# First four blocks of a layer side by side, their weights split ahead of the norm, and no weight split on GpSimd

## The chip, the cores and the metric

The kernel runs on one core of one Trainium2 chip. A core has a matrix engine (TensorE, PE), a vector engine (VectorE, DVE), an activation engine (ScalarE, ACT), a general engine (GpSimd, POOL) and an engine that only issues DMAs here (SyncE, SP). Each works through its own list of instructions in order and waits on semaphores for the others. The metric is the device time of one execution in microseconds (us), as a median of several runs. A difference of less than 0.2%, about 5 us, is not told from no change.

## The reference

Four layers of a transformer-like network run over 512 tokens of width 1024, in float32. In short:

```python
# first_block: two layers, each with a LayerNorm behind the mixer and behind the FFN
h = layer_norm(ALPHA * h + s5_mixer(h), ...)              # state-space model, then a GLU
h = layer_norm(ALPHA * h + swiglu_ffn(h, w_gu, w_down))   # hidden width 2816
h = layer_norm(ALPHA * h + stick_breaking_mixer(h), ...)  # 16 heads
h = layer_norm(ALPHA * h + swiglu_ffn(h, w_gu, w_down))
# second block: two layers with an RMS norm ahead of each part
h = h + mixer_even(rms_norm(h))      # gated MLP beside dilated attention
h = h + conv_ffn(rms_norm(h))        # SwiGLU FFN with a causal convolution of 3 taps
h = h + mixer_odd(rms_norm(h))       # gated linear attention, 4 heads
h = h + conv_ffn(rms_norm(h))
```

## The kernel before, in words

The activations stand transposed: 8 tiles `v[m]` of 128 features by 512 tokens. Eight stages follow each other: ssm, ffn0, stick, ffn1, even (gated MLP, then dilated attention), conv0, gla, conv1.

Float32 accuracy comes from splitting. An activation tile is `xh` (rounded) plus `xl` (the rest); a weight block of 128x1024 is `wh` plus `wl`. `mm3` takes three matmuls for each of 8 tiles k: `xh` with `wh`, `xl` with `wh`, `xh` with `wl`. An output block of 128x512 thus needs 24 matmuls of 512 columns, or 48 of 256 if it is worked half by half.

`weight()` makes a block ready: SP loads 512 KB into `wr` (2 buffers), ACT rounds it to `wh` (L207), and a subtraction gives `wl` (L210). The subtraction runs on DVE, apart from 44 blocks for which it runs on GpSimd: all of dilated attention's (`lo_pool`), and the first few after each norm, counted by `AHEAD`. `wh` and `wl` have 4 buffers each.

`linear()` runs a layer's input blocks. With `split_first=4` the first four are worked half by half: all of block 0's first half, then block 1's, and so on, and then the second halves. The convolution FFNs have no such start. `out_blocks()` runs the output blocks and the norm: the last `nl` blocks half by half, and behind each half its norm. For LayerNorm that is `ln_half`: `colsum` sums the columns on PE, DVE works out the inverse root of the variance in some 14 instructions on `small` tiles (`rstd`, L363 to L370), `spread` makes `diag` operands (L394) which PE multiplies by ones to bring the row to all partitions (L396), and then each of 8 tiles is subtracted from and multiplied (L410, L411), scaled and shifted by ACT, rounded to `xh` by ACT (L214), and its rest `xl` taken by DVE (L215). For the RMS norm (`rms_half`) only the scale's row is made, and it is applied where the next layer's blocks are read out; the next tiles are made ahead of it by `scaled` (L352, L353).

The order of the instructions on each engine is set by a scheduler at build time, except that the SSM stage's steps follow a written list, `SSM_STEPS`, and the attentions lists of their own. In `SSM_STEPS` a letter is a kind of step and a digit the tile or group: P powers of the state matrix; m, q, n, N products of powers and inputs on DVE; A, B, C, X matmuls or their preparation; W and w the load and split of a GLU weight; G the GLU's matmuls.

Of the kernel before, what the change touches and what calls it, by code (L numbers as in the profile page):

```python
# [98 lines left out]
class Kern:  # L99
    def __init__(self, tc, ins, out, ctx):  # L100
        self.tc, self.nc, self.i, self.out = tc, tc.nc, ins, out
        self.g = ctx.enter_context(tc.tile_pool(name="glob", bufs=1))
# [4 lines left out]
        self.lo_pool = False
        self.nw = 0
        self.nb = 0
        self.boundary = ()  # L110
# [151 lines left out]
    def out_blocks(self, blocks, xh, xl, kind, g=None, b=None, alpha=1.0, rg=None, nl=1):  # L262
# [1519 lines left out]
```

## Time and profile before

| what | value |
|---|---|
| median of 3 runs | 2511.8 us (2509.65 to 2515.39) |
| the profiled execution's own time | 2507.85 us |
| its span | 2506.1 us |
| granted TensorE clock, mean of the span | 0.988 of full speed |
| GpSimd busy | 117.9 us |
| ScalarE busy | 1004.9 us |

The profile is of one execution; its own time is 3.95 us below the median of the runs. The span is the time from its first to its last instruction. Busy time counts an engine's instructions; the clock is that which TensorE was granted, 1.00 being 2.4 GHz and 0.50 being 1.2 GHz.

### The profile page before, as it was taken

The numbers are of one execution on the slowest core, as the hardware profiler recorded it, in microseconds if no ns is written. First come the engines' busy times: TensorE is split into PE (matmuls) and PEld (weight loads), VectorE is DVE, ScalarE is ACT, GpSimd is POOL, SyncE is SP. The second block draws the span as 40 slices with busy tenths as digits, with TensorE's granted clock in tenths as the row PEclk, the third lists the DMA queues.
The fourth block names the chain that finished last, engine by engine and source line by source line (L and its number), as shares of the span: only waits on it lengthen the run. The fifth ranks groups of instructions, "written<-read, shape, count | busy, mean of one in ns | idle before, by whom it ended". The sixth has DMA issues, their size and how long they took to land. (4 is left out here: it accounts for less than half of the span.)

```text
span 2506.1 us, 31148 instructions
## 1 busy us (share of the span) xinstructions
PE 2417.5 (96%) x12296; PEld 2006.6 (80%) x12300; DVE 1445.8 (58%) x2512; ACT 1004.9 (40%) x1552; POOL 117.9 (5%) x106
## 2 busy tenths in 40 slices
PE   5899999999999999999998899999999999999999
PEld 4788888888877788888876678888888888788888
DVE  8955733343777884333377787656435667666531
ACT  4853422322555643232244454333324554333321
POOL 0000100000100010000023202000000000100000
PEclk9899999999999999999999999999999999999999
DMA  3332232233211113223322112222332122222332
GB/s 104 71 102 97 68 101 96 97 93 95 84 60 60 45 58 118 98 95 94 94 82 76 46 39 91 94 101 94 94 99 78 68 85 76 84 97 96 97 108 73
DMA packets 99378, 213.52 MB, mean 85 GB/s; under 512 B 44528, under 2 KB 45168, under 8 KB 99232
## 3 DMA queue, kind: packets, MB, share of 16 engines
q1 hardware_dynamic: 99232, 211.53, 26.5%
q8 instruction: 97, 1.59, 0.3%
q14 instruction: 49, 0.40, 0.1%
HBM read 207.04 MB, written 2.10 MB: 83 GB/s over the span
## 5 line engine op out<-in xcount | busy, mean ns | idle before, releaser
L207 ACT ACTIVATE wh<-wr 128x1024 fp32r<-128x1024 f32 (+1 forms) x385 | 400.3, 1041 | 1010.8 <-PE mm L230 392.6
L210 DVE TENSOR_TENSOR wl<-wr,wh 128x1024 fp32r<-128x1024 f32 (+1 forms) x341 | 408.8, 1199 | 450.4 <-ACT wh L207 449.5
L230 PE MATMUL mm<-xl,wh 128*128 128x512 f32 (+1 forms) x1144 | 439.9, 385 | 0.0
L229 PE MATMUL mm<-xh,wh 128*128 128x512 f32 (+1 forms) x1144 | 439.2, 387 | 0.2 <-ACT scr L1309 0.2
L231 PE MATMUL mm<-xh,wl 128*128 128x512 f32 (+1 forms) x1144 | 438.4, 384 | 0.0
L230 PE MATMUL acc<-xl,wh 128*128 128x512 f32 (+1 forms) x888 | 336.0, 379 | 6.6 <-DVE xl L215 6.4
L229 PE MATMUL acc<-xh,wh 128*128 128x512 f32 (+1 forms) x888 | 337.2, 380 | 1.2 <-ACT xh L214 1.0
L231 PE MATMUL acc<-xh,wl 128*128 128x512 f32 (+1 forms) x888 | 336.0, 378 | 0.0
L229 PEld LDWEIGHTS mm<-xh,wh 128*128 128x128 f32 x1144 | 216.5, 190 | 42.7 <-issue 2.8
L230 PEld LDWEIGHTS mm<-xl,wh 128*128 128x128 f32 x1144 | 217.3, 190 | 40.9 <-issue 0.7
L231 PEld LDWEIGHTS mm<-xh,wl 128*128 128x128 f32 x1144 | 217.2, 190 | 40.6 <-issue 0.4
L230 PEld LDWEIGHTS acc<-xl,wh 128*128 128x128 f32 x888 | 167.2, 189 | 38.4 <-DVE xl L215 7.6
L210 POOL TENSOR_TENSOR wl<-wr,wh 128x1024 fp32r<-128x1024 f32 (+1 forms) x44 | 105.1, 2391 | 1901.6 <-ACT wh L207 1839.4
L229 PEld LDWEIGHTS acc<-xh,wh 128*128 128x128 f32 x888 | 167.6, 189 | 32.6 <-ACT xh L214 1.4
L231 PEld LDWEIGHTS acc<-xh,wl 128*128 128x128 f32 x888 | 167.5, 189 | 31.0
L229 PE MATMUL acc<-hh,wh 128*128 128x512 f32 (+1 forms) x396 | 145.0, 366 | 1.0 <-DVE v L327 1.0
L229 PE MATMUL mm<-hh,wh 128*128 128x512 f32 (+1 forms) x396 | 145.0, 366 | 0.5 <-DVE v L327 0.5
L230 PE MATMUL acc<-hl,wh 128*128 128x512 f32 (+1 forms) x396 | 145.2, 367 | 0.0
L230 PE MATMUL mm<-hl,wh 128*128 128x512 f32 (+1 forms) x396 | 144.8, 366 | 0.0
L231 PE MATMUL mm<-hh,wl 128*128 128x512 f32 (+1 forms) x396 | 144.7, 365 | 0.0
L231 PE MATMUL acc<-hh,wl 128*128 128x512 f32 (+1 forms) x396 | 144.7, 365 | 0.0
L229 PEld LDWEIGHTS acc<-hh,wh 128*128 128x128 f32 x396 | 74.6, 188 | 13.5 <-DVE v L327 1.4
(468 smaller groups left out, 3693.1 us busy)
## 6 DMA issues: line engine op xcount, KB each, us to landing
wr<-down_dram SPq DMA_DIRECT2D x64, 448.0 KB, 3.3
wr<-gu_g_dram SPq DMA_DIRECT2D x44, 512.0 KB, 3.2
wr<-gu_u_dram SPq DMA_DIRECT2D x44, 512.0 KB, 3.2
wr<-gate_dram SPq DMA_DIRECT2D x44, 512.0 KB, 3.2
wr<-up_dram SPq DMA_DIRECT2D x44, 512.0 KB, 3.2
wr<-down_dram SPq DMA_DIRECT2D x32, 512.0 KB, 3.5
wr<-sb_qkv_dram SPq DMA_DIRECT2D x24, 512.0 KB, 3.2
wr<-glu_dram SPq DMA_DIRECT2D x16, 512.0 KB, 3.3
```

The source lines that it names most:

```text
L207: nc.scalar.activation(hi[:, :cols], raw[:, :cols], AF.Copy)
L210: (nc.gpsimd if pool else nc.vector).tensor_sub(lo[:, :cols], raw[:, :cols], hi[:, :cols])
L229: nc.tensor.matmul(ps[:, c0:c1], wh[:, s], xh[k][:, c0:c1], start=st, stop=False)
L230: nc.tensor.matmul(ps[:, c0:c1], wh[:, s], xl[k][:, c0:c1], start=False, stop=False)
L231: nc.tensor.matmul(ps[:, c0:c1], wl[:, s], xh[k][:, c0:c1], start=False, stop=en)
```

## The change

GpSimd splits no weights any more: all `wl` come from DVE. `FIRST` names each stage's first four blocks (none for gla). `prepare()` loads and splits them ahead of their layer: where the last blocks go half by half, two of the four ahead of these and two in the norm between its rows and its tiles; where `nl` is 0, all four behind the last block. `wh` and `wl` get 5 buffers each. `mm3_side` works four blocks side by side: for each tile k the three matmuls of each of the four, in halves (`parts=2`) for ffn0, ffn1 and stick, over the full 512 columns for the convolution FFNs, which had no joint start before. Blocks 3 and 4 take `aux` banks of PSUM. `ln_half` becomes `ln_rows` and `ln_apply`, the first half applied in two parts; ACT makes `xh` straight from the scaled tile. The output blocks of even and gla are all full-width (`nl` 2 to 0). The list of SSM steps is new; three tags lose a buffer (`scr` 9 to 8, `tst` 4 to 3, `BC` 4 to 3).

```diff
 SSM_STEPS = (
-    "q1 i0 i1 W2 q0 W3 m0 P0 A0 m1 K0 A0 P1 A1 K0 Z0 A0 K1 P2 D1 A1 D0 a1 D2 P3 i2 A1 K1 b1 n0 K1 i3 B1 D3 c1 K0 "
...
+    "P0 i0 i1 W0 m0 W2 P1 q0 P2 A0 m1 K0 A0 P3 K0 A0 q1 K0 i2 B0 e0 m2 q2 A1 s0 n0 A2 K1 N0 Z0 A1 K2 n1 D0 A2 K1 "
...
-AHEAD = (4, 3, 4, 6, 7, 1, 7, 0)
+FIRST = {
+    "ffn0": [(n, 0, f) for f in (0, 1) for n in ("gu_g", "gu_u")],
+    "stick": [("sb_qkv", m) for m in (8, 0, 16, 9)],
+    "ffn1": [(n, 1, f) for f in (0, 1) for n in ("gu_g", "gu_u")],
+    "even": [("ev_v", u) for u in range(4)],
+    "conv0": [(n, 0, f) for f in (0, 1) for n in ("gate2", "up2")],
+    "conv1": [(n, 1, f) for f in (0, 1) for n in ("gate2", "up2")],
+}
...
     def scr(self, dt=F32):
-        return self.gt("scr", [P, T], dt, bufs=9)
+        return self.gt("scr", [P, T], dt, bufs=8)
...
-    def weight(self, ap, cols=1024):
-        nc = self.nc
+    def weight(self, *key, ap=None, cols=1024):
+        nc = self.nc
+        if key and key in self.early:
+            return self.early.pop(key)
         raw = self.wt("wr", F32, 2)
-        nc.sync.dma_start(raw[:, :cols], ap)
-        hi, lo = self.wt("wh", F32R, 4), self.wt("wl", F32R, 4)
+        nc.sync.dma_start(raw[:, :cols], self.i[key[0]][key[1:]] if ap is None else ap)
+        hi, lo = self.wt("wh", F32R, 5), self.wt("wl", F32R, 5)
         nc.scalar.activation(hi[:, :cols], raw[:, :cols], AF.Copy)
-        self.nw += 1
-        pool = self.lo_pool or self.nw in self.boundary
-        (nc.gpsimd if pool else nc.vector).tensor_sub(lo[:, :cols], raw[:, :cols], hi[:, :cols])
+        nc.vector.tensor_sub(lo[:, :cols], raw[:, :cols], hi[:, :cols])
         return hi, lo
+
+    def prepare(self, n):
+
+        for key in self.coming[:n]:
+            self.early[key] = self.weight(*key)
+        self.coming = self.coming[n:]
...
+    def mm3_side(self, pss, ws, xh, xl, parts=1):
+
+        nc = self.nc
+        n = T // parts
+        for c0 in range(0, T, n):
+            c = slice(c0, c0 + n)
+            for k in range(NM):
+                s = slice(k * P, (k + 1) * P)
+                for ps, ((wh, wl), _, _) in zip(pss, ws):
+                    nc.tensor.matmul(ps[:, c], wh[:, s], xh[k][:, c], start=k == 0, stop=False)
+                    nc.tensor.matmul(ps[:, c], wl[:, s], xh[k][:, c], start=False, stop=False)
+                    nc.tensor.matmul(ps[:, c], wh[:, s], xl[k][:, c], start=False, stop=k == NM - 1)
+
+    def linear(self, blocks, xh, xl, evict, side=0, parts=1, group=1):
 
         n = len(blocks)
         i = 0
-        if split_first:
-            ws = [blocks[j]() for j in range(split_first)]
-            pss = [self.bank() for _ in range(split_first)]
-            for h in (0, 1):
-                for j in range(split_first):
-                    self.mm3(pss[j], ws[j], xh, xl, h * HALF, (h + 1) * HALF)
-            for j in range(0, split_first, group):
+        if side:
+            ws = [blocks[j]() for j in range(side)]
+            pss = [self.bank() if j < 2 else self.aux() for j in range(side)]
+            self.mm3_side(pss, [w for w, in ws], xh, xl, parts)
+            for j in range(0, side, group):
                 evict(j, pss[j:j + group])
-            i = split_first
+            i = side
...
+            if m == NM - nl - 1:
+                self.prepare(2 if nl else 4)
         last = range(NM - nl, NM)
         ws, pss = {}, {}
-        for h in (0, 1):
+        if not nl and rms:
+            for h in (0, 1):
+                self.rms_half(h, acc2)
+        for h in (0, 1) if nl else ():
             c = slice(h * HALF, (h + 1) * HALF)
             for m in last:
                 if h == 0:
@@ -339,12 +365,16 @@
                 if h == 0:
                     for m in range(NM):
                         next_tiles(m)
-                self.ln_half(h, acc1, acc2, g, b, nxh, nxl, rg)
+                    rows0 = self.ln_rows(0, acc1, acc2)
+                    self.prepare(4)
+                    self.ln_apply(0, range(4), rows0, g, b, nxh, nxl, rg)
+                else:
+                    self.ln_apply(0, range(4, NM), rows0, g, b, nxh, nxl, rg)
+                    rows1 = self.ln_rows(1, acc1, acc2)
+                    self.ln_apply(1, range(NM), rows1, g, b, nxh, nxl, rg)
             if rms:
                 self.rms_half(h, acc2)
         self.xh, self.xl = nxh, nxl
-        self.boundary = range(self.nw + 1, self.nw + 1 + AHEAD[self.nb])
-        self.nb += 1
...
-    def ln_half(self, h, acc1, acc2, g, b, nxh, nxl, rg):
-        nc, v = self.nc, self.v
-        c = slice(h * HALF, (h + 1) * HALF)
+    def ln_rows(self, h, acc1, acc2):
+
+        nc = self.nc
         d = self.colsum([acc1, acc2], (2 * h, 2 * h + 1))
         q = self.small(2)
         nc.vector.tensor_mul(q, d[:, :2], d[:, :2])
         nc.vector.scalar_tensor_tensor(q, d[:, 2:4], 1e-5, q, op0=ALU.add, op1=ALU.subtract)
-        r = self.rstd(q, 2)
-        db, rb = self.spread([d[:, :2], r])
-        for m in range(NM):
+        return self.spread([d[:, :2], self.rstd(q, 2)])
+
+    def ln_apply(self, h, ms, rows, g, b, nxh, nxl, rg):
+        nc, v = self.nc, self.v
+        c = slice(h * HALF, (h + 1) * HALF)
+        for m in ms:
             y = self.scr()[:, :HALF]
-            nc.vector.tensor_sub(y, v[m][:, c], db)
-            nc.vector.tensor_mul(y, y, rb)
+            nc.vector.tensor_sub(y, v[m][:, c], rows[0])
+            nc.vector.tensor_mul(y, y, rows[1])
             gm, bm = g[:, m:m + 1], b[:, m:m + 1]
             if rg is None:
-                nc.scalar.activation(v[m][:, c], y, AF.Identity, scale=gm, bias=bm)
-                self.split(v[m][:, c], nxh[m][:, c], nxl[m][:, c])
-                continue
+                nc.scalar.activation(nxh[m][:, c], y, AF.Identity, scale=gm, bias=bm)
             nc.scalar.activation(v[m][:, c], y, AF.Identity, scale=gm, bias=bm)
-            self.scaled(m, c, rg, nxh, nxl)
+            if rg is None:
+                nc.vector.tensor_sub(nxl[m][:, c], v[m][:, c], nxh[m][:, c])
+            else:
+                self.scaled(m, c, rg, nxh, nxl)
...
-            self.linear(blocks, self.xh, self.xl, evict, split_first=4 if conv is None else 0, group=2)
+            self.linear(blocks, self.xh, self.xl, evict, side=4, parts=2 if conv is None else 1, group=2)
...
-    BC = 4
+    BC = 3
...
-            for h in (0, 1):
-                for w, ps in zip(ws, pss):
-                    self.mm3(ps, w, xh, xl, h * HALF, (h + 1) * HALF)
+            self.mm3_side(pss, [w for w, in ws], xh, xl, 2)
...
-    def attention(self, pairs, first, project, weigh, done, mask, order, units, lo_pool=False):
-
-
-        self.lo_pool = lo_pool
...
-            self.out_linear(self.simple_blocks("ev_wo", NM), oh, ol, "rms", rg=self.nfg[0], nl=2)
+            self.out_linear(self.simple_blocks("ev_wo", NM), oh, ol, "rms", rg=self.nfg[0], nl=0)
...
-            self.out_linear(self.simple_blocks("od_wo", NM), oh, ol, "rms", rg=self.nfg[1], nl=2)
+            self.out_linear(self.simple_blocks("od_wo", NM), oh, ol, "rms", rg=self.nfg[1], nl=0)
...
-        for s in stages:
+        for n, s in enumerate(stages):
+            k.coming = FIRST.get(stages[n + 1], []) if n + 1 < len(stages) else []
```

Three pairs of excerpts show how the instructions stand on two engines. First PE at the start of ffn0: `acc` and `mm` are the PSUM banks of its first two blocks, `xh_2168` the first tile's rounded part, `wh_2454` and `wh_2460` the weights. Before:

```order
L229 MATMUL acc_2476<-xh_2168,wh_2454 128x256
L230 MATMUL acc_2476<-xl_2169,wh_2454 128x256
L231 MATMUL acc_2476<-xh_2168,wl_2455 128x256
L229 MATMUL acc_2476<-xh_2170,wh_2454 128x256
L229 MATMUL mm_2477<-xh_2168,wh_2460 128x256
L230 MATMUL mm_2477<-xl_2169,wh_2460 128x256
L230 MATMUL acc_2476<-xl_2171,wh_2454 128x256
L231 MATMUL acc_2476<-xh_2170,wl_2455 128x256
L229 MATMUL acc_2476<-xh_2172,wh_2454 128x256
L230 MATMUL acc_2476<-xl_2173,wh_2454 128x256
```

After, with the names and lines of the changed kernel (`xh_2178`, `wh_2057` and `wh_2063`):

```order
L252 MATMUL acc_2474<-xh_2178,wh_2057 128x256
L253 MATMUL acc_2474<-xh_2178,wl_2058 128x256
L254 MATMUL acc_2474<-xl_2179,wh_2057 128x256
L252 MATMUL mm_2475<-xh_2178,wh_2063 128x256
L253 MATMUL mm_2475<-xh_2178,wl_2064 128x256
L254 MATMUL mm_2475<-xl_2179,wh_2063 128x256
L252 MATMUL acc_2474<-xh_2180,wh_2057 128x256
L253 MATMUL acc_2474<-xh_2180,wl_2058 128x256
L252 MATMUL mm_2475<-xh_2180,wh_2063 128x256
L253 MATMUL mm_2475<-xh_2180,wl_2064 128x256
L254 MATMUL acc_2474<-xl_2181,wh_2057 128x256
L254 MATMUL mm_2475<-xl_2181,wh_2063 128x256
```

Block 1 ran on to its second and third tile as soon as they were there, with block 2 in the gaps. Now the blocks alternate tile by tile, and the `wl` product stands ahead of the `xl` product.

Next DVE in the norm between SSM and ffn0, around the two `diag` operands of its first half. Before:

```order
L370 SCALAR_TENSOR_TENSOR small_2209<-small_2206,small_2204 128x2
L394 TENSOR_SCALAR diag_2218<-ident_58,small_2209 128x128
L394 TENSOR_SCALAR diag_2221<-ident_58,small_2209 128x128
L410 TENSOR_TENSOR scr_2224<-v_739,aux_2211 128x256
L411 TENSOR_TENSOR scr_2224<-scr_2224,aux_2211 128x256
L410 TENSOR_TENSOR scr_2230<-v_799,aux_2211 128x256
L411 TENSOR_TENSOR scr_2230<-scr_2230,aux_2211 128x256
L410 TENSOR_TENSOR scr_2236<-v_857,aux_2211 128x256
L327 TENSOR_TENSOR v_1316<-v_1316,mm_2100 128x256
L411 TENSOR_TENSOR scr_2236<-scr_2236,aux_2211 128x256
L215 TENSOR_TENSOR xl_2169<-v_739,xh_2168 128x256
L410 TENSOR_TENSOR scr_2242<-v_946,aux_2211 128x256
```

After (`wl_2237` and `wl_2243` are the lower parts of ffn0's third and fourth weight):

```order
L302 TENSOR_TENSOR acc_369_1864<-acc_369_1864,v_1240 128x256
L400 SCALAR_TENSOR_TENSOR small_2219<-small_2216,small_2214 128x2
L214 TENSOR_TENSOR wl_2237<-wr_2234,wh_2236 128x1024
L424 TENSOR_SCALAR diag_2228<-ident_58,small_2219 128x128
L424 TENSOR_SCALAR diag_2231<-ident_58,small_2219 128x128
L443 TENSOR_TENSOR scr_2246<-v_673,aux_2221 128x256
L353 TENSOR_TENSOR v_1310<-v_1310,mm_2110 128x256
L444 TENSOR_TENSOR scr_2246<-scr_2246,aux_2221 128x256
L443 TENSOR_TENSOR scr_2252<-v_738,aux_2221 128x256
L214 TENSOR_TENSOR wl_2243<-wr_2240,wh_2242 128x1024
L450 TENSOR_TENSOR xl_2179<-v_673,xh_2178 128x256
L444 TENSOR_TENSOR scr_2252<-scr_2252,aux_2221 128x256
```

A split of 128x1024 now stands right ahead of the two `diag` instructions, and another between the second tile's subtraction and the first tile's `xl`. Before, GpSimd had them.

Last PE at the entry of conv0, where even's last output block ends and the RMS norm's row is spread (`aux` from `diag`). Before, `mm_12781` is the last output block and `mm_12950` conv0's first:

```order
L231 MATMUL mm_12781<-oh_12466,wl_12778 128x256
L229 MATMUL mm_12781<-oh_12495,wh_12777 128x256
L230 MATMUL mm_12781<-ol_12496,wh_12777 128x256
L396 MATMUL aux_12839<-diag_12840,ones_1436 128x128
L396 MATMUL aux_12839<-diag_12843,ones_1436 128x128
L231 MATMUL mm_12781<-oh_12495,wl_12778 128x256
L229 MATMUL mm_12950<-xh_12537,wh_12946 128x512
L230 MATMUL mm_12950<-xl_12538,wh_12946 128x512
```

After, `mm_12906` and `acc_12907` are conv0's first two blocks:

```order
L253 MATMUL acc_12907<-xh_12652,wl_12821 128x512
L254 MATMUL acc_12907<-xl_12653,wh_12820 128x512
L252 MATMUL mm_12906<-xh_12691,wh_12814 128x512
L253 MATMUL mm_12906<-xh_12691,wl_12815 128x512
L426 MATMUL aux_12861<-diag_12862,ones_1434 128x128
L426 MATMUL aux_12861<-diag_12865,ones_1434 128x128
L411 MATMUL aux_12869<-cst_63,acc_2317_12501 128x1 x2
L254 MATMUL mm_12906<-xl_12692,wh_12814 128x512
L252 MATMUL acc_12907<-xh_12691,wh_12820 128x512
L253 MATMUL acc_12907<-xh_12691,wl_12821 128x512
L254 MATMUL acc_12907<-xl_12692,wh_12820 128x512
L252 MATMUL mm_12906<-xh_12730,wh_12814 128x512
```

The spread stood within the last output block's second half. It now stands among the full-width matmuls of the next stage's first blocks.

## Rows read from the trace of the kernel before

**Rows 1.** The page: busy time of PE and DVE over the span

```profile
PE 2417.5 (96%) x12296; PEld 2006.6 (80%) x12300; DVE 1445.8 (58%) x2512; ACT 1004.9 (40%) x1552; POOL 117.9 (5%) x106
```

**Rows 2.** Windows of 50 us: length, busy time (instructions) by engine, clock, DMA share, GB/s

```profile
50.00:100.00 50.00, 37.24 (x359) 34.24 (x358) 42.91 (x54) 35.27 (x68) 0.45 (x4) 0.86 0.31 71
250.00:300.00 50.00, 44.48 (x327) 42.66 (x326) 37.81 (x101) 24.82 (x47) 7.09 (x3) 0.93 0.13 44
300.00:350.00 50.00, 50.00 (x222) 41.43 (x221) 20.69 (x22) 16.93 (x22) 0.00 (x0) 1.00 0.36 117
900.00:950.00 50.00, 44.24 (x297) 41.37 (x296) 37.29 (x86) 27.68 (x49) 7.33 (x3) 0.93 0.19 64
1250.00:1300.00 50.00, 46.14 (x276) 39.95 (x275) 32.02 (x77) 18.05 (x31) 10.94 (x5) 1.00 0.28 94
1300.00:1350.00 50.00, 41.14 (x173) 32.01 (x171) 45.77 (x93) 27.80 (x50) 15.01 (x6) 0.94 0.22 74
```

**Rows 3.** Waits of PE: us in total, times, longest

```profile
PE aux L396 <- DVE diag L394: 11.0, 8, 2.2
...
PE acc L230 <- DVE xl L215: 6.4, 4, 2.6
...
PE aux L1227 <- ACT vnh L214: 5.0, 1, 5.0
...
PE aux L1325 <- DVE small L1318: 2.8, 2, 2.2
...
PE aux L381 <- DVE acc L281: 2.3, 1, 2.3
```

**Rows 4.** Timeline of DVE, 257 to 271 us: start, duration

```profile
258.27 2.65 DVE L394 TENSOR_SCALAR diag<-ident,small 128x128 f32<-128x128 f32 x2
...
265.06 2.42 DVE L215 TENSOR_TENSOR xl<-v,xh 128x256 fp32r<-128x256 f32 x1 [0.48 <-ACT xh L214]
...
267.40 0.41 DVE L410 TENSOR_TENSOR scr<-v,aux 128x256 f32<-128x256 f32 x1
...
268.40 2.90 DVE L215 TENSOR_TENSOR xl<-v,xh 128x256 fp32r<-128x256 f32 x2
```

**Rows 5.** Timeline of POOL, the same stretch

```profile
264.80 2.40 POOL L210 TENSOR_TENSOR wl<-wr,wh 128x1024 fp32r<-128x1024 f32 x1 [4.16 <-ACT wh L207]
...
268.34 2.34 POOL L210 TENSOR_TENSOR wl<-wr,wh 128x1024 fp32r<-128x1024 f32 x1 [1.14 <-ACT wh L207]
```

**Rows 6.** Timeline of DVE in the gated MLP, 1330 to 1350 us

```profile
1335.02 5.70 DVE L1206 TENSOR_TENSOR scr<-scr,ev_ln_g 128x512 f32<-128x512 f32 x2
...
1343.96 1.28 DVE L1206 TENSOR_TENSOR scr<-scr,ev_ln_g 128x512 f32<-128x512 f32 x2
```

**Rows 7.** Timeline of PE, 255 to 275 us: in brackets the wait before

```profile
260.78 0.71 PE L396 MATMUL aux<-diag,ones 128*128 128x128 f32 x4 [2.15 <-DVE diag L394]
...
271.02 0.39 PE L230 MATMUL acc<-xl,wh 128*128 128x256 f32 x1 [2.62 <-DVE xl L215]
```

**Rows 8.** Windows of PE alone: length, busy (instructions), clock, DMA

```profile
261.00:265.00 4.00, 4.00 (x23) 0.59 0.40 135
271.00:275.00 4.00, 3.98 (x22) 0.62 0.40 131
280.00:298.20 18.20, 17.59 (x142) 1.00 0.00 1
1350.00:1356.00 6.00, 5.80 (x24) 0.67 0.25 87
1428.00:1436.00 8.00, 8.00 (x35) 0.72 0.00 0
1540.00:1545.00 5.00, 4.67 (x18) 0.67 0.38 112
```

**Rows 9.** The page: groups of the weight split, by engine

```profile
L210 DVE TENSOR_TENSOR wl<-wr,wh 128x1024 fp32r<-128x1024 f32 (+1 forms) x341 | 408.8, 1199 | 450.4 <-ACT wh L207 449.5
...
L210 POOL TENSOR_TENSOR wl<-wr,wh 128x1024 fp32r<-128x1024 f32 (+1 forms) x44 | 105.1, 2391 | 1901.6 <-ACT wh L207 1839.4
```

More of the change, by code (lines that the diff above doesn't have):

```diff
@@ L106, in __init__ @@
         self.fresh, self.taken = [], {}
[L107 to L110, printed above, removed]
+        self.early, self.coming = {}, []
         self.consts()
@@ L231, in mm3 @@
                 nc.tensor.matmul(ps[:, c0:c1], wl[:, s], xh[k][:, c0:c1], start=False, stop=en)
-    def linear(self, blocks, xh, xl, evict, split_first=0, group=1):
+    def mm3_side(self, pss, ws, xh, xl, parts=1):
[10 more added lines that the diff above has]
+    def linear(self, blocks, xh, xl, evict, side=0, parts=1, group=1):
         n = len(blocks)
         i = 0
-        if split_first:
-            ws = [blocks[j]() for j in range(split_first)]
-            pss = [self.bank() for _ in range(split_first)]
-            for h in (0, 1):
-                for j in range(split_first):
-                    self.mm3(pss[j], ws[j], xh, xl, h * HALF, (h + 1) * HALF)
-            for j in range(0, split_first, group):
+        if side:
[3 more added lines that the diff above has]
+            for j in range(0, side, group):
                 evict(j, pss[j:j + group])
-            i = split_first
+            i = side
         while i < n:
@@ L460, in block @@
             def block(name, f):
-                return lambda: [(self.weight(self.i[name][layer, f]), 0, 8)]
+                return lambda: [(self.weight(name, layer, f), 0, 8)]
             blocks = [b for f in range(FT) for b in (block(gname, f), block(uname, f))]
@@ L484, in evict @@
                 self.split(s, hh[f], hl[f])
-            self.linear(blocks, self.xh, self.xl, evict, split_first=4 if conv is None else 0, group=2)
+            self.linear(blocks, self.xh, self.xl, evict, side=4, parts=2 if conv is None else 1, group=2)
             def dblock(m):
-                return lambda: [(self.weight(self.i[dname][layer, m][:, k0 * P:(k0 + nk) * P], nk * P), k0, nk)
+                return lambda: [(self.weight(ap=self.i[dname][layer, m][:, k0 * P:(k0 + nk) * P], cols=nk * P), k0, nk)
                                 for k0, nk in FSPLIT]
@@ L494, in simple_blocks @@
     def simple_blocks(self, name, n):
-        return [(lambda m=m: [(self.weight(self.i[name][m]), 0, 8)]) for m in range(n)]
+        return [(lambda m=m: [(self.weight(name, m), 0, 8)]) for m in range(n)]
     def vexp(self, x, sp, minus1=True):
@@ L874, in ssm @@
                                  self.ident[:, None, :].to_broadcast([P, 16, P]), AF.Copy, scale=0.0)
-            self.tst = [self.pt(f"tst{k}", [P, 8, 65]) for k in range(4)]
+            self.tst = [self.pt(f"tst{k}", [P, 8, 65]) for k in range(3)]
             for t in self.tst:
@@ L918, in ssm @@
                     elif f == "W":
-                        raw, w = self.wt("wr", F32, 2), [self.wt(n, F32R, 4) for n in ("wh", "wl")]
+                        raw, w = self.wt("wr", F32, 2), [self.wt(n, F32R, 5) for n in ("wh", "wl")]
                         self.nc.sync.dma_start(raw, self.i["glu"][(o // 2) + 8 * (o % 2)])
@@ L925, in ssm @@
                         self.nc.vector.tensor_sub(w[1], raw, w[0])
-                        self.nw += 1
                         fps[o] = self.mm()
@@ L1065, in scores, with attention @@
         return z
-    def attention(self, pairs, first, project, weigh, done, mask, order, units, lo_pool=False):
-        self.lo_pool = lo_pool
+    def attention(self, pairs, first, project, weigh, done, mask, order, units):
         st = [{} for _ in range(pairs)]
@@ L1097, in attention @@
                         done(hp, s["o"])
-        self.lo_pool = False
     def stick(self):
@@ L1152, in token_proj @@
         nc = self.nc
-        ws = [self.weight(u) for u in units]
+        ws = [self.weight(*u) for u in units]
         pss = [self.bank() for _ in range(4)]
@@ L1180, in early @@
                 self.mm3(pu[-1], w, self.xh, self.xl)
-        pv = self.token_proj([i["ev_v"][u] for u in range(4)], self.xh, self.xl)
+        pv = self.token_proj([("ev_v", u) for u in range(4)], self.xh, self.xl)
         with self.phase("big") as self.big:
@@ L1355, in first @@
                 project(hp, st[hp], n)
-        self.attention(4, first, project, weigh, done, mask, EVEN_STEPS, EVEN_UNITS, lo_pool=True)
+        self.attention(4, first, project, weigh, done, mask, EVEN_STEPS, EVEN_UNITS)
     def even(self):
@@ L1412, in gla_gate @@
         nc = self.nc
-        w = self.weight(self.i["od_ga"], P)
+        w = self.weight(ap=self.i["od_ga"], cols=P)
         ps = self.mm()
@@ L1430, in gla_values @@
         nc = self.nc
-        ws = [self.weight(self.i["od_v"][pair, u]) for u in range(4)]
+        ws = [self.weight("od_v", pair, u) for u in range(4)]
         for tb in range(4):
```

14 rows, old and new, of the table SSM_STEPS are left out of this document.

## The prediction

> **What bounds the kernel now.** I looked first at the page: TensorE (PE) is busy 96% of the span and VectorE (DVE) 58% [rows 1]. So what any change can win is PE's idle time, some 88 us of 2506, and the time that PE spends at a lower clock. The 50-us windows say where those are: a stretch in the middle of a layer holds 222 matmuls of 512 columns and PE is busy all of it, while 50–100 us (the state-space mixer), 250–300, 900–950 and 1250–1350 us hold 37 to 46 us of PE work, some at clock 0.86 to 0.94 [rows 2]. Apart from the first, these windows are layer ends: the norm needs the last block, the next layer needs the norm.
>
> The waits of PE, grouped by what ended them, name the norm's own chain: the `diag` operands of the spread 11.0 us in 8 waits, `xl` 6.4 us in 4, then `vnh` in the gated MLP 5.0, `small` in dilated attention 2.8, and others [rows 3]. All come from DVE or, as `vnh`, from ScalarE (ACT) behind DVE.
>
> Why is DVE late there? Going to its rows at one layer end: a `diag` pair takes 2.65 us at 258.27 and an `xl` 2.42 at 265.06, while the 256-wide subtract at 267.40 takes 0.41; the next `xl` pair takes 2.90 [rows 4]. GpSimd (POOL) runs a weight split at just these moments: 264.80 to 267.20 and 268.34 to 270.68 [rows 5]; each long DVE instruction ends within 0.3 us of its split's end. In the gated MLP two multiplies take 5.70 us beside POOL's two splits and 1.28 us without [rows 6]. So a split on POOL doesn't run beside DVE there: it holds a DVE instruction for about 2.0 to 2.2 us. PE waits 2.15 us for that `diag` and 2.62 for that `xl` [rows 7], and after either its granted clock is 0.59 or 0.62 for 4 us, mostly the lower level (1.2 of 2.4 GHz) [rows 8].
>
> **The change part by part.**
>
> *Splits.* 44 leave POOL (2391 ns each) and join DVE's queue (1199 ns each) [rows 9]: DVE gains 44 × 1.2 = 52.8 us of its own work. What it loses are the holds: at most 44 × 2.0 = 88 us if each split holds one instruction, as both of rows 5 do, at least nothing. I take three in four, 66 us, since some splits fall where DVE is idle or reads PSUM. DVE's load falls by some 13 us; with no hold at all it would rise by 53, and the busiest window's 45.8 of 50 us [rows 2] would be the place that feels it.
>
> The Trainium skill bears on this in both directions (Perfetto Trace Analysis, "Optimizing Scalar/DVE Operations"): where DVE is saturated, moving work to GpSimd may make sense, though the two share an SBUF read port and it might not help. The GPSIMD Engine Reference ("Key points") names the contention: DVE instructions in a 2-port mode or with two SBUF inputs. By the first half of the rule, the six splits that POOL does in 1300–1350 us would cost DVE 7 us more there, and the sum below would lose the 5 us of that place; rows 6 agree with the second half.
>
> *Layer end, LayerNorm* (first output block pairs of the next layer, 2 halves). The matmuls stay 256 wide there, and their order changes: four blocks take tile 0, then tile 1, so that PE needs one new tile for 12 matmuls, 12 × 0.124 = 1.5 us (17.59 us for 142 in 280–298 [rows 8]), where one block took 3, 0.37 us. DVE makes a tile in three instructions of 0.41 (subtract, multiply, `xl`) [rows 4], 1.25 us: PE no longer outruns it. Ahead of the `diag` now stands one DVE split, and one more among the first tiles. At SSM→ffn0, hence: of the wait of 2.15, 1.2 stay, 0.95 go; of the 2.62, 1.2 stay, 1.4 go; of the clock's loss, 4 × 0.41 + 4 × 0.38 = 3.2 us [rows 8], I take back half, 1.6, since shorter waits may still lower it. Gain 4.0; bounds: nothing (the waits only move) and all, 5.5 idle + 3.2 = 8.7. Stick→ffn1 (900–950: 5.8 idle, clock 0.93 [rows 2]) is built alike: 4.0, bounds 0 and 8.7. ffn0→stick is not among the stretches with much idle time: 0.5, bounds −1 and 1.5. The two weights split ahead of the last blocks, and the other two in the norm, replace loads that came behind it; two more buffers (`wh`, `wl`) hold them. Their DMAs keep their number and size, and the DMA share in 250–300 is 0.13 [rows 2]. The new direct ACT write of `xh` takes one step from each tile's chain and adds no instruction.
>
> *ffn1→gated MLP* (1250–1350: 3.9 + 8.9 idle [rows 2]). Waits of 2.3 (`acc`) and 5.0 (`vnh`) [rows 3] stand out. Before `vnh` the multiplies are held 5.70 − 1.28 = 4.4 us [rows 6]; with two DVE splits, 2.4, in that place, 2.0 go. Of the 2.3, 1.2 stay, 1.1 go; clock 0.67 over 6 us [rows 8] gives 1.0 of its 2.0; of the smaller waits, 5.5 us together, I take 0.9: 5. Bounds 0 and 12.
>
> *Dilated attention.* Eight splits move into DVE's in-order queue, 9.6 us, against eight holds of 2.0. PE's 2.8 us of waits for `small` [rows 3] and the 2.2 us that clock 0.72 costs over the next 8 [rows 8] are at stake, 5 us; I take half, 2.5, as the splits can stand ahead of the same chain, and 0.5 for lesser waits: 3. Bounds −1 and 6.
>
> *Conv layers' entries* (from the dilated layer and from gated linear attention). The last two output blocks go full-width. A pair of 256-wide matmuls takes 0.248 us, one 512-wide 0.225 [rows 8, 2], so 48 × 0.023 = 1.1 us per entry. The norm's chain moves under the first blocks of the next layer (PE's order: colsum, then 13 full matmuls, 2.9 us, before the spread), and the held `diag` wait (2.2 at most [rows 3]) and clock 0.67 over 5 us, 1.7 [rows 8], go: 5.0 in all. I keep 2 back for splits on DVE in the chain: 3 each, bounds 1 and 5. Half a microsecond comes from gated linear attention's own start, whose one split moves too.
>
> *SSM.* The written-out order is new, with three buffers for two tiles that had four and eight scratch tiles for nine. In 50–100 us DVE is busy 42.9 of 50 and PE 37.2 [rows 2]: DVE sets the pace, and its work is the same. Its 7.1 idle us are the bound of a gain; 1.3 us more work (one step of 1.2 us and part of a power) stands ahead of the first matmul, so +6 at best. Fewer buffers could as well double the idle time: −8. The new table lets the weight splits' loads wait behind the third output tile but drops two table switches of ACT. I take +2.
>
> *At nothing:* POOL's idle time, and the reordered product terms (`wl` before `xl`): both lie beside PE's work; if `wl` came late it would cost its 1.2 us, once per entry.
>
> **Sum:** SSM 2 + 4 + 0.5 + 4 + 5 + 3 + 3 + 3 + 0.5 = 25 us. Against the profiled execution's 2507.85 (span 2506.1, 1.75 around it) that is 2482.9. The median of the runs shown is 2511.8, 3.95 above the profiled one; the forecast as a median is 2486.8, rounded **2487**.
>
> **The rivals.**
>
> *The waits only move* (small gain). DVE executes in order: a split stands ahead of `diag` and waits for ACT's `wh`, which waits for the load. Then the layer ends and attention give nothing; conv entries 6, SSM 2, 0.5 remain: 2503. For it: DVE at 45.8 of 50. Against it: 1.2 us takes the place of 2.0 to 2.2.
>
> *All of it goes.* PE finds every tile ready: the upper bounds 8.7 + 8.7 + 1.5 + 12 + 6 + 5 + 5 + 0.5 with SSM's 2 make 49, so 2462. Against it: after the last block the chain of the norm must still run before the second half.
>
> *The clock stays low* (no change). PE now paces tile by tile with DVE, 1.5 against 1.25 us, so short waits come between groups of 12 matmuls. If these held the clock at its lower level through the first halves of four blocks at three entries, each would lose 96 × (0.21 − 0.12) = 8.6 us (rows 8: 0.124 at clock 1.00; 0.21 lies midway between 0.181, 22 in 3.98 us at 0.62, and twice 0.124), 26 in all, one more than the sum: 2513. Rows 8 show the fall after waits over 2 us, and the 0.61 us of idle in 280–298 left it at 1.00. The Trainium skill describes such a loss (TensorE: Matmul & The Clock Gate, "A second HAM failure mode: psum-queue depth-cycling"): micro-idles between groups make the clock swing. No row here shows it.
>
> *A late load stops DVE* (slower). In the norm the third and fourth weight need a raw buffer of the two; if their load lands after the split's turn, everything behind it on DVE stops: `diag`, all tiles, evictions of the blocks. At the price of the 2.62-us wait and half of 3.2 for the clock, 4.2 us twice in each of four norms, 34 us stand against 25: 2521. It decides from 3.1 us per split. For it: DVE mostly waited for ACT's `wh` before a split (449.5 of 450.4 us [rows 9]). Against: the first two loads come three blocks earlier, 16 us.
>
> **How the numbers follow.** Forecast (2477 to 2498, one of its larger terms lost or doubled): 0.64. Only moved: 0.14. All: 0.08. Clock: 0.06. Late load: 0.08. About 5 us, 0.2%, is what a measurement here can tell from no change. Faster by more: 0.64 + 0.08 + 0.10 of "only moved" = 0.82; within: 0.04 + 0.06 = 0.10; slower: 0.08. The range 2466 to 2508 holds the forecast with a larger gain in part, and "only moved", and leaves out most of the full gain and the last two.
>
> **What would show it.** Right: no DVE instruction of `diag`, `xl` or `small` over 0.8 us; `diag` and `xl` waits of PE together under 8 us (now 17.4); `vnh` near 3; DVE busy 1425 to 1445 us; windows as 250–300 with 47 or more of PE at clock 0.96 or above. Wrong: waits of PE for `wl`; DVE waiting over 2 us before a split inside a norm; PE busy below 37 us in 50–100 us; clock under 0.8 in a stretch of short waits.

## The result, and the profile after

| what | before | after |
|---|---|---|
| median | 2510.73 us (4 runs) | 2474.44 us (4 runs, 2473.41 to 2475.27) |
| ratio | | 0.9852, 95% interval 0.9835 to 0.9869 |
| profiled execution, span | 2507.85, 2506.1 | 2473.41, 2471.7 |
| clock, mean of the span | 0.988 | 0.992 |

The change takes 36 us, 1.5%. The forecast was 25 us (2487), with a range of 2466 to 2508. The range holds the result, but the narrower band of 2477 to 2498, to which the prediction gave 0.64, doesn't. On the page of the changed kernel, PE's busy time and the single group of weight splits answer to [rows 1, 9]:

```profile
PE 2405.6 (97%) x12200; PEld 1993.5 (81%) x12204; DVE 1415.8 (57%) x2544; ACT 1005.5 (41%) x1542; POOL 14.0 (1%) x61
...
L214 DVE TENSOR_TENSOR wl<-wr,wh 128x1024 fp32r<-128x1024 f32 (+1 forms) x385 | 461.7, 1199 | 448.4 <-ACT wh L213 443.9
```

DVE makes 44 splits more and is busy 30 us less. PE's idle time falls from 88.6 to 66.1 us, and its busy time by 11.9 us. The mean clock, 0.992 after 0.988, can make up about 10 of these (an estimate: 0.004 of 2500 us). The windows of the changed kernel, against [rows 2]:

```profile
50.00:100.00 50.00, 41.44 (x401) 38.28 (x401) 44.78 (x58) 41.30 (x77) 0.34 (x3) 0.90 0.43 89
250.00:300.00 50.00, 47.38 (x321) 43.92 (x321) 35.11 (x93) 29.19 (x50) 0.00 (x0) 0.97 0.21 68
900.00:950.00 50.00, 48.70 (x286) 44.15 (x286) 29.82 (x72) 26.29 (x43) 0.00 (x0) 0.93 0.25 83
1250.00:1300.00 50.00, 45.24 (x264) 37.65 (x264) 40.41 (x110) 29.04 (x60) 1.09 (x1) 1.00 0.28 85
1300.00:1350.00 50.00, 46.24 (x222) 36.86 (x222) 37.41 (x93) 24.77 (x42) 4.35 (x14) 0.93 0.26 85
```

Its waits of PE, against [rows 3]; the waits for `diag`, `xl` and `vnh`, 22.4 us there, are 4.1 here. Some waiting has moved to ACT: at the layer ends the waits for `xh` come to 5.4 us, 1.7 in the kernel before, and the 3.1 us for `scr` are new:

```profile
PE aux L91 <- DVE m L91: 24.2, 3, 21.8
PE mm L239 <- ACT scr L1338: 3.1, 1, 3.1
...
PE mm L1190 <- ACT xh L382: 2.3, 2, 2.1
PE aux L426 <- DVE diag L424: 2.0, 4, 1.0
...
PE mm L252 <- ACT xh L447: 1.9, 2, 1.0
PE acc L252 <- ACT xh L447: 1.2, 2, 0.9
...
PE acc L254 <- DVE xl L450: 0.9, 2, 0.7
PE mm L254 <- DVE xl L450: 0.9, 2, 0.7
...
PE aux L1256 <- ACT vnh L224: 0.3, 1, 0.3
```

Where did the 34.4 us of span go? The timeline of PE gives the first matmul on `zh` (SSM's output blocks), on `hh` (an FFN's output blocks) and on `oh` (output blocks of even and gla). These marks cut the span into stretches. Before:

```profile
216.18 0.39 PE L229 MATMUL acc<-zh,wh 128*128 128x512 f32 x1
...
515.96 0.39 PE L229 MATMUL acc<-hh,wh 128*128 128x512 f32 x1
...
1158.62 0.39 PE L229 MATMUL acc<-hh,wh 128*128 128x512 f32 x1
...
1482.29 0.47 PE L229 MATMUL mm<-oh,wh 128*128 128x512 f32 x1
...
1783.29 0.39 PE L229 MATMUL mm<-hh,wh 128*128 128x512 f32 x1
...
2083.20 0.50 PE L229 MATMUL mm<-oh,wh 128*128 128x512 f32 x1
...
2381.60 0.39 PE L229 MATMUL mm<-hh,wh 128*128 128x512 f32 x1
```

After, the same marks in the same order:

```profile
209.11 0.39 PE L239 MATMUL acc<-zh,wh 128*128 128x512 f32 x1
...
504.11 0.39 PE L239 MATMUL mm<-hh,wh 128*128 128x512 f32 x1
...
1144.33 0.39 PE L239 MATMUL acc<-hh,wh 128*128 128x512 f32 x1
...
1452.40 0.39 PE L239 MATMUL mm<-oh,wh 128*128 128x512 f32 x1
...
1751.06 0.39 PE L239 MATMUL acc<-hh,wh 128*128 128x512 f32 x1
...
2053.76 0.50 PE L239 MATMUL mm<-oh,wh 128*128 128x512 f32 x1
...
2347.16 0.39 PE L239 MATMUL mm<-hh,wh 128*128 128x512 f32 x1
```

The lead grows 7.1, 11.9, 14.3, 29.9, 32.2, falls to 29.4 and ends at 34.4 us. So, by stretch, with the forecast's terms in brackets: SSM 7.1 (2); SSM→ffn0 4.8 (4); ffn0→stick and stick→ffn1 2.4 (4.5); gated MLP and dilated attention 15.6 (8); conv0's entry 2.3 (3); gated linear attention −2.8 (0.5); conv1's entry 5.0 (3). That is one profile each, and single stretches differ by some us between executions (gated linear attention: −2.8 here, 0.1 in a second profile of the changed kernel), so the parts were tried alone.

### The profile page after: what moved, and what is told of

Its sections match the earlier page's. It is cut to its first block, busy times and chain, and to the rows that moved or that the text cites. A ratio compares the mean times of both kernels' runs of the same rounds, so it can differ in the third digit from the quotient of the medians.

```text
span 2471.7 us, 30857 instructions
## 1 busy us (share of the span) xinstructions
PE 2405.6 (97%) x12200; PEld 1993.5 (81%) x12204; DVE 1415.8 (57%) x2544; ACT 1005.5 (41%) x1542; POOL 14.0 (1%) x61
## 5 line engine op out<-in xcount | busy, mean ns | idle before, releaser
L214 DVE TENSOR_TENSOR wl<-wr,wh 128x1024 fp32r<-128x1024 f32 (+1 forms) x385 | 461.7, 1199 | 448.4 <-ACT wh L213 443.9
L239 PE MATMUL mm<-xh,wh 128*128 128x512 f32 x1016 | 398.9, 393 | 3.5 <-ACT scr L1338 3.1
L241 PE MATMUL mm<-xh,wl 128*128 128x512 f32 x1016 | 398.5, 392 | 0.0
L240 PE MATMUL mm<-xl,wh 128*128 128x512 f32 x1016 | 398.3, 392 | 0.0
L239 PE MATMUL acc<-xh,wh 128*128 128x512 f32 x760 | 296.7, 390 | 0.0
L240 PE MATMUL acc<-xl,wh 128*128 128x512 f32 x760 | 296.3, 390 | 0.0
L241 PE MATMUL acc<-xh,wl 128*128 128x512 f32 x760 | 296.0, 389 | 0.0
L240 PEld LDWEIGHTS mm<-xl,wh 128*128 128x128 f32 x1016 | 191.3, 188 | 39.5 <-issue 0.2
L241 PEld LDWEIGHTS mm<-xh,wl 128*128 128x128 f32 x1016 | 191.4, 188 | 39.0 <-issue 0.6
L239 PEld LDWEIGHTS acc<-xh,wh 128*128 128x128 f32 x760 | 143.0, 188 | 29.4
L239 PEld LDWEIGHTS mm<-hh,wh 128*128 128x128 f32 x396 | 74.6, 189 | 13.6 <-DVE v L353 1.4
```

The lines of the kernel that those rows point to most:

```text
L214: nc.vector.tensor_sub(lo[:, :cols], raw[:, :cols], hi[:, :cols])
L239: nc.tensor.matmul(ps[:, c0:c1], wh[:, s], xh[k][:, c0:c1], start=st, stop=False)
L240: nc.tensor.matmul(ps[:, c0:c1], wh[:, s], xl[k][:, c0:c1], start=False, stop=False)
L241: nc.tensor.matmul(ps[:, c0:c1], wl[:, s], xh[k][:, c0:c1], start=False, stop=en)
```

## The experiments

The theory: a split on GpSimd holds a VectorE instruction that works on SBUF, PE waits for that one, and moving the splits makes most of the gain. The main rival: the new order (blocks side by side, weights early) makes it.

**Only the splits.** The kernel before, one line changed.

```diff
-        (nc.gpsimd if pool else nc.vector).tensor_sub(lo[:, :cols], raw[:, :cols], hi[:, :cols])
+        nc.vector.tensor_sub(lo[:, :cols], raw[:, :cols], hi[:, :cols])
```

> The kernel before with all 44 GpSimd splits done by VectorE and nothing else changed. Theory (a split on GpSimd holds a VectorE instruction for 2.0 to 2.2 us, and that is what PE waits for): all but the SSM stage's 7 us, the conv layers' full width and part of the norms' gain appears: 16 to 24 us less than before, about 2491; the gated MLP and dilated attention give 12 to 16 of it. Rival (side-by-side blocks and early splits remove the waits, and the splits' engine does not matter): 0 to 5 us, 2506 to 2511, with waits of PE for wl or diag at the norms in place of the old ones.

Measured: 2485.86 us against 2511.41, ratio 0.9897 (0.9882 to 0.9913): 25.6 us less, a little over the theory's 16 to 24; the rival's 0 to 5 is out. By the marks its profile gains 10.6 us in the gated MLP and dilated attention, under the 12 to 16 expected there, and 3.8, 4.1, 1.6 and 4.1 at ffn0, ffn1, conv0 and conv1. Its page:

```profile
PE 2412.9 (97%) x12300; PEld 2005.6 (81%) x12300; DVE 1422.7 (57%) x2556; ACT 1004.8 (40%) x1552; POOL 15.9 (1%) x62
```

With 44 × 1.2 = 52.8 us of splits added, DVE's busy time falls by 23.1 from [rows 1]. The holds were thus 75.9 us, 1.73 per split on average.

**The splits twice.** All splits on VectorE, and GpSimd does 960 columns of the same 44 again, for a tile that nobody reads.

```diff
-        (nc.gpsimd if pool else nc.vector).tensor_sub(lo[:, :cols], raw[:, :cols], hi[:, :cols])
+        nc.vector.tensor_sub(lo[:, :cols], raw[:, :cols], hi[:, :cols])
+        if pool:
+            n = min(cols, 960)
+            wj = self.w.tile([P, 960], F32, name=self.nm("wj"), tag="wj", bufs=1)
+            nc.gpsimd.tensor_sub(wj[:, :n], raw[:, :n], hi[:, :n])
```

> The kernel before with all 44 splits on VectorE, and GpSimd making 960 of the 1024 columns of the same 44 a second time into a tile that nobody reads. VectorE's work is that of the first experiment; only GpSimd's access beside it is added. Theory (GpSimd's access holds VectorE's instructions): the gain of 25.6 us is lost and more, since VectorE now has the splits and the holds: 2508 to 2530, with diag and xl instructions over 2 us. Rival (the order of VectorE's queue or the earlier end of the splits made the gain, not the access): 2484 to 2490.

Measured: 2541.54 us against 2509.98, ratio 1.0120 (1.0106 to 1.0133). That is 56 us over the first experiment, more than the theory's 2508 to 2530. Its page (PE, DVE) and its first waits at the norm:

```profile
PE 2426.3 (96%) x12300; PEld 2013.9 (79%) x12300; DVE 1499.7 (59%) x2556; ACT 1005.2 (40%) x1552; POOL 130.3 (5%) x106
```

```profile
PE aux L400 <- DVE diag L398: 16.0, 9, 4.0
PE aux L1231 <- ACT vnh L218: 6.4, 1, 6.4
```

DVE runs the same 2556 instructions, in the same order, 77.0 us longer: 1.75 per GpSimd instruction. So the access itself holds DVE, not the order of the queue. By the marks the loss against the first experiment lies at the layer ends and in the gated MLP and dilated attention (24.6 us), and none of it in gated linear attention. One more thing came with the second splits: they keep the raw weight, and 16 loads waited for that, as the DMA queue's waits show:

```profile
SPq L205 <- POOL wj L214: 33.3, 16, 2.1
```

How much of the 56 us is theirs was not tried apart.

**The splits twice, in the middle of a layer.** The three-part kernel below with 44 second splits in blocks 8 to 18 of the two convolution FFNs, gate and up.

```diff
-                return lambda: [(self.weight(self.i[name][layer, f]), 0, 8)]
+                return lambda: [(self.weight(self.i[name][layer, f], twice=conv is not None and 8 <= f < 19), 0, 8)]
```

> The three-part kernel (splits on VectorE, SSM list, full-width last blocks; 2474.5 before) with 44 second splits on GpSimd as in the experiment that made splits twice, but in the middle of the two convolution layers' input blocks, where PE has full blocks to run and VectorE is less than 80% busy. Theory (a hold costs time only where PE waits for VectorE's chain): VectorE's busy time rises by some 77 us as there, the time stays within 4 us: 2472 to 2479. Rival (a hold costs PE wherever it falls, by the late eviction or the late wl): 20 to 55 us more, 2495 to 2530.

Measured: 2472.59 us; the same kernel without them, at another time, 2474.5; the ratios to the kernel before are 0.9853 (0.9838 to 0.9869) and 0.9852 (0.9837 to 0.9868). DVE's busy time on the page is 1496.9 against 1421.0: 75.9 us of holds, and no time lost. Two windows of this kernel, then the same windows without second splits:

```profile
1600.00:1650.00 50.00, 50.00 (x222) 41.44 (x221) 45.51 (x37) 18.60 (x23) 22.59 (x10) 1.00 0.27 95
1650.00:1700.00 50.00, 50.00 (x222) 41.40 (x222) 45.97 (x38) 18.59 (x23) 20.37 (x9) 1.00 0.28 100
```

```profile
1600.00:1650.00 50.00, 50.00 (x222) 41.41 (x222) 29.36 (x36) 18.55 (x24) 0.00 (x0) 1.00 0.29 95
1650.00:1700.00 50.00, 50.00 (x223) 41.41 (x221) 31.14 (x38) 18.91 (x25) 0.00 (x0) 1.00 0.29 96
```

DVE goes from 29.4 to 45.5 of 50 us with 10 GpSimd instructions, and PE doesn't miss one of 222 matmuls. In this place the holds cost nothing, since PE doesn't wait for DVE there. Groups of this kernel (busy, mean ns of one) show which instructions are held:

```profile
L209 DVE TENSOR_TENSOR wl<-wr,wh 128x1024 fp32r<-128x1024 f32 x320 | 457.4, 1430 | 256.5 <-ACT wh L207 255.8
...
L477 DVE SCALAR_TENSOR_TENSOR scr<-scr,cst,scr 128x511 f32<-128x511 f32 x44 | 48.6, 1106 | 1.8 <-ACT scr L476 1.8
...
L475 DVE TENSOR_TENSOR scr<-mm,rrow 128x512 f32<-128x512 f32 x22 | 15.1, 685 | 29.5 <-PE mm L233 27.4 <-ACT rrow L445 2.1
```

The first is DVE's own weight split, the second a step of the convolution; both read two tensors in SBUF, and without the second splits they took 1225 and 746 ns. Most of the holds fall on the weight split, 65.7 us. The mean of the second hides two kinds: of the 44 convolution steps 8 run beside GpSimd, at 2.74 us each, and the other 36 take 0.74. The last group, with one operand in PSUM, had 692; 8 of its 22 run beside GpSimd and take 0.68 us. This is what the Trainium skill says of the shared interface (GPSIMD Engine Reference, "Key points": contention with two SBUF inputs); the trace agrees.

**Only the SSM list**, with its three buffers, in the kernel before.

```diff
-    "q1 i0 i1 W2 q0 W3 m0 P0 A0 m1 K0 A0 P1 A1 K0 Z0 A0 K1 P2 D1 A1 D0 a1 D2 P3 i2 A1 K1 b1 n0 K1 i3 B1 D3 c1 K0 "
+    "P0 i0 i1 W0 m0 W2 P1 q0 P2 A0 m1 K0 A0 P3 K0 A0 q1 K0 i2 B0 e0 m2 q2 A1 s0 n0 A2 K1 N0 Z0 A1 K2 n1 D0 A2 K1 "
...
-    BC = 4
+    BC = 3
```

> The kernel before with the new list of SSM steps and the three buffers that go with it, nothing else. Theory (the list alone makes the SSM stage 7 us shorter, by filling VectorE's idle time): 7 us less, about 2504, the first matmul of the stage's output blocks at 209 us. Rival (the stage gains from the fifth weight buffer and the smaller scratch, the list costs as in the prediction's bounds): within 2 us of before.

Measured: 2502.43 us against 2511.41, ratio 0.9964 (0.9951 to 0.9977): 9.0 us less, over the theory's 7, and SSM's output blocks begin at 205.79 in place of 216.18. The list with its buffers makes the gain; the rival's 2 us is out. The stage in windows, before:

```profile
0.00:25.00 25.00, 0.67 (x3) 0.70 (x4) 20.59 (x100) 9.39 (x11) 1.68 (x21) 1.00 0.54 183
25.00:50.00 25.00, 21.75 (x142) 21.30 (x141) 22.75 (x46) 13.81 (x36) 0.45 (x4) 0.86 0.27 35
50.00:75.00 25.00, 14.85 (x120) 12.83 (x118) 20.38 (x27) 16.07 (x32) 0.23 (x2) 0.86 0.24 74
75.00:100.00 25.00, 22.39 (x239) 21.41 (x240) 22.53 (x28) 19.20 (x37) 0.23 (x2) 0.86 0.38 68
```

and with the new list:

```profile
0.00:25.00 25.00, 2.28 (x8) 1.96 (x9) 21.64 (x112) 9.39 (x11) 1.64 (x20) 1.00 0.49 173
25.00:50.00 25.00, 22.74 (x170) 22.20 (x169) 24.52 (x39) 13.72 (x38) 0.34 (x3) 1.00 0.26 40
50.00:75.00 25.00, 19.73 (x227) 18.09 (x225) 24.59 (x34) 23.28 (x45) 0.34 (x3) 0.93 0.43 73
75.00:100.00 25.00, 20.85 (x162) 19.42 (x163) 22.03 (x26) 19.52 (x35) 0.00 (x0) 0.86 0.46 111
```

DVE works 6.5 us more in these 100 us and PE 5.9, and the clock, at 0.86 for 75 us before, gives 25 × (0.14 + 0.07) = 5.3 us. These overlap and don't add up. The changed kernel keeps less of it: its two profiles gain 7.1 and 7.8 us at this mark, this one 10.4. Which of its other parts takes the difference was not tried.

**36 splits back on GpSimd** in the changed kernel: the 24 early ones and dilated attention's 12.

```diff
+            self.lo_pool = True
             self.early[key] = self.weight(*key)
+            self.lo_pool = False
```

> The changed kernel with 36 splits on GpSimd again: the 24 that are made ready ahead of a layer and the 12 of dilated attention. Theory (holds): the waits come back, 36 holds of 2 us less 36 splits of 1.2 us on VectorE, and PE loses 10 to 18 us against the changed kernel: 2484 to 2492. Rival (side-by-side blocks give PE so much slack per tile that holds cost nothing): 2474 to 2478.

Measured: 2486.74 us against 2511.41, ratio 0.9899 (0.9884 to 0.9913): 12 us over the changed kernel, as the theory had it. PE waits again, 5.8 us for `diag` and 3.2 for `vnh`. Blocks side by side don't cover a hold.

**No blocks side by side** in the changed kernel.

```diff
-            self.mm3_side(pss, [w for w, in ws], xh, xl, parts)
+            for c0 in range(0, T, T // parts):
+                for j in range(side):
+                    self.mm3(pss[j], ws[j], xh, xl, c0, c0 + T // parts)
```

> The changed kernel with its first four blocks one after the other again, half by half (in the convolution layers over the full width), everything else as changed. Theory (holds on VectorE were the main cause; the order gives little): 2 to 6 us more than the changed kernel, 2476 to 2480. Rival (the order by tiles is the main cause of the gain at the norms): 10 to 16 us more, 2484 to 2490, with PE waits for xl and xh at ffn0, stick and ffn1.

Measured: 2472.09 us (2468.58 to 2478.99), ratio 0.9846 (0.9827 to 0.9865). No loss, and not even the theory's 2 to 6 us: the order by tiles gives nothing that can be measured. The rival's 10 to 16 is out.

**No early weights**, and **neither**. `prepare` makes nothing ready; the second kernel has the last experiment's edit too.

```diff
-        for key in self.coming[:n]:
+        for key in []:
```

> The changed kernel without early weights: the first four blocks' weights are loaded and split by their own layer, as all others, and still worked side by side. Theory (early weights are needed only because four blocks side by side want four weights at once): 4 to 10 us more than the changed kernel, 2478 to 2484, PE waiting for wl or wh at the starts of ffn0, stick, ffn1. Rival (loads are early enough from the scheduler's own order): 2472 to 2477.

> The changed kernel with neither early weights nor side-by-side blocks; what is left of the change is the splits on VectorE, the SSM list, the full-width last blocks, five weight buffers and the norm applied in parts. Theory (those two parts carry no gain; early weights cost some 3 us by putting splits ahead of the norm's diag): 2467 to 2474. Rival (each of the two can go alone but not both, since one covers for the other): 2478 to 2490, with waits of PE at the norms.

Measured: 2469.2 us (2467.47 to 2472.07), ratio 0.9833 (0.9819 to 0.9846), beside the changed kernel with 2472.49, ratio 0.9844 (0.9830 to 0.9857). With neither: 2469.99, ratio 0.9844 (0.9830 to 0.9858). The theory that early weights are needed falls, and its rival stands: side-by-side blocks don't need them, and the time is even a little under the rival's 2472 to 2477. With neither, the theory's 2467 to 2474 holds, and the rival, that one covers for the other, falls. Whether early weights cost the 3 us between the two medians is not settled, as the intervals overlap. The control, the 2472.49 above, came out as expected:

> The changed kernel again, beside the others of this call: 2472 to 2477 for any theory.

**Only the full width** of the last two blocks of the two RMS layers (`nl` 2 to 0), in the kernel before.

```diff
-            self.out_linear(self.simple_blocks("ev_wo", NM), oh, ol, "rms", rg=self.nfg[0], nl=2)
+            self.out_linear(self.simple_blocks("ev_wo", NM), oh, ol, "rms", rg=self.nfg[0], nl=0)
```

> The kernel before with the last two output blocks of the two RMS layers full-width and nothing else. Prediction's own term: 1.1 us for each of two layers from the wider matmuls, and the norm's chain moves under the next layer's blocks, 2 to 5 us less in all: 2506 to 2508. Rival (the half-by-half blocks hid the norm's chain, which is now bare): 2 to 6 us more.

Measured: 2511.66 us against 2509.24, ratio 1.0011 (1.0002 to 1.0020): no gain, and a small loss rather, as the rival had it. It is under the 5 us that are told from no change, but its profile has it in the right places: by the marks it loses 2.2 and 2.1 us at the entries of conv0 and conv1. At conv0's entry PE waits 2.3 us for `diag` and 1.8 for the column sum's `acc`, 2.1 and 0.4 in the kernel before: the held chain is barer than it was.

**Three parts**: splits on VectorE, SSM list, full width, in the kernel before; no early weights, no side-by-side blocks, four buffers.

> The kernel before with three parts only: all splits on VectorE, the new SSM list with its three buffers, and the full-width last blocks of the two RMS layers. No early weights, no side-by-side blocks, four weight buffers. Theory (these parts carry the gain; measured alone the first two gave 25.6 and 9.0 us, the third is worked out as 2): 34 to 37 us less than before, 2474 to 2477, like the changed kernel. Rival (early weights and side-by-side blocks carry part of it and the parts do not add up): 2481 or more.

Measured: 2474.5 us, ratio 0.9852 (0.9837 to 0.9868), the changed kernel's own ratio. The first two parts alone add up to 25.6 + 9.0 = 34.6 of its 36 us. By the marks its profile gains 2.5 and 4.9 us at the entries of conv0 and conv1, where the splits alone gained 1.6 and 4.1. With the holds gone, the full width thus gives 0.9 and 0.8 us there (one profile each), where with them it lost 2.2 and 2.1.

## Why the prediction was right, and where its sizes were off

**The mechanism was right.** GpSimd's splits held DVE, and PE waited for that. The holds came to 75.9, 77.0 and 75.9 us for 44 splits in three kernels, against 66 forecast: 1.73 to 1.75 us each. In the kernel with 36 back on GpSimd it is 55.6 us, 1.54 each (DVE 1428.2 us busy, 12.4 more than the changed kernel's, with 36 × 1.2 us less work). The gain of 36 us lies outside the forecast's own band all the same. What is missing from the 25 us are 7.0 in the SSM term and some 5 in the terms of the splits.

**What the holds cost PE was mis-sized.** The forecast left a 1.2-us split standing in each chain: its terms for the norms, the gated MLP, attention and the conv entries without the full width come to 21 us; the splits alone gave 25.6. The norms came out as forecast in that kernel's profile (3.8 and 4.1 against 4 and 4.5); the gated MLP and attention (10.6 against 8) and the conv entries (5.8 against 3.8) were taken too low. In the gated MLP it let 2.0 of the 5.0 us for `vnh` go; 4.7 went, since DVE's two multiplies now take 1.28 us with no split between. For dilated attention it counted eight splits; there are twelve (`AHEAD` sums to 32 of 44).

**The SSM term failed.** It said 2 us, at best 6, since DVE's 7.1 idle us were the bound and 1.3 us more work stood ahead of the first matmul. The list alone gave 9.0. The first matmul comes earlier, not later (PE's first wait is 21.8 us, before 24.3), because one product of 1.22 us stands ahead of it where three did. DVE's products before, and in the changed kernel:

```profile
20.69 3.50 DVE L84 TENSOR_TENSOR m<-pw,bc 128x1024 f32<-128x1024 f32 x3
```

```profile
20.42 1.22 DVE L91 TENSOR_TENSOR m<-pw,bc 128x1024 f32<-128x1024 f32 x1
```

And the bound was read from one window, 50 to 100 us. In the four windows above, 0 to 100 us, DVE is idle 13.8 us before and 7.2 with the new list: it fills 6.5 us, most of the gain. The clock, 5.3 us, was left out too; how much of the 9.0 is due to it stays open.

**The full-width term hung on another part.** Worked out as 1.1 us per entry from matmul spacing, it costs 2.4 us when made alone, since the norm's chain, still held, then stands bare. With the splits moved it gives 0.9 and 0.8, near the term. Most of the conv entries' gain (2.3 and 5.0 in the profile, 6 forecast) comes from the splits: 1.6 and 4.1.

**Side-by-side blocks** were credited with keeping PE from outrunning DVE. Without them nothing is lost.

**The rivals.** Most waits went and did not move: PE has none for `wl`. The part that moved is the 3.7 us more for `xh` and the 3.1 for `scr` above. No load stopped DVE. The clock's rival shows at two entries: behind short waits (0.85 us at the longest) the changed kernel's clock drops at ffn0 (0.97 in 250–300) and at ffn1, where it is at its lower level, 1.2 GHz, for 4 us. The longest wait ahead of ffn1, then windows of PE alone (the last three are of gated linear attention, for the last section):

```profile
897.00 0.39 PE L252 MATMUL mm<-xh,wh 128*128 128x256 f32 x1 [0.85 <-ACT xh L447]
```

```profile
903.00:907.00 4.00, 4.00 (x19) 0.50 0.02 6
1928.00:1932.00 4.00, 3.73 (x22) 1.00 0.38 131
1932.00:1936.00 4.00, 4.00 (x14) 0.60 0.00 0
1936.00:1940.00 4.00, 4.00 (x14) 0.54 0.02 4
```

This fits the Trainium skill (TensorE: Matmul & The Clock Gate, "A second HAM failure mode: psum-queue depth-cycling"): micro-idles between groups of matmuls can cost the clock; the falls here, behind waits of 0.85 us and less, are of that kind, though no run tried the cause alone. The window 900–950 has 0.93 as before the change, so the 1.6 us that the term took back from the clock did not come. That would be most of the 2.1 us by which ffn0→stick→ffn1 fell short (an estimate from one profile).

**The signs named in advance:** of `diag`, `xl` and `small` one instruction is left over 0.8 us, an `xl` of 1.25 beside a GpSimd instruction that is no split, which fits the hold:

```profile
1277.03 1.25 DVE L383 SCALAR_TENSOR_TENSOR xl<-v,cst,xh 128x256 fp32r<-128x256 f32 x1
```

```profile
1276.90 1.09 POOL L1217 TENSOR_SCALAR_AFFINE_SELECT wsr<-wsr 128x1024 f32<-128x1024 f32 x1 [646.58 <-DVE scr L444]
```

The `diag` and `xl` waits are 3.8 us, under 8; that for `vnh` is 0.3, where 3 was named; 250–300 us is at 47.4 and 0.97. DVE's busy time, 1415.8, is under the 1425 to 1445, as the holds were larger. Of the signs against, the low clock behind short waits appeared.

## What to carry to other kernels

Before work is moved to GpSimd to relieve VectorE, look for VectorE instructions that stretch while GpSimd runs: here 2.4 us on GpSimd cost VectorE 1.73 us of hold on average, more than the 1.2 us that the same split takes on VectorE. What such a hold costs depends on its place: 44 second splits cost nothing in the middle of a layer and 56 us at the layer ends. A part can also depend on another: the full width lost time with the holds and won some without them. And a change of many parts is best taken apart: one line and one list carried most of this one's gain.

## What the runs showed of the hardware that was not expected

A held VectorE instruction stands until the GpSimd one is done, and then runs: in [rows 4, 5] `xl` ends at 267.48, 0.28 us after the split. That the average is 1.73 to 1.75 us for 2.4 to 2.6 us of GpSimd comes from instructions that start after GpSimd has, and from splits that meet none. VectorE instructions with a PSUM operand pass in 685 ns against 692. The clock fell in gated linear attention (0.60 and 0.54 in the windows of the section before) after a longest wait of 0.27 us, in a run of 256-column matmuls on 64 or 128 rows; the same instructions stayed at 1.00 in the profile of the kernel before. It is the 2.8 us lost there. A second profile of the changed kernel doesn't show the loss; those of the kernels without side-by-side blocks and with neither part do (3.4 and 2.8 us). What decides it stays open.
